# Seven block products of sums in place of eight in most of a SwiGLU down projection

## The chip, the cores and the metric

The kernel runs on one core of a Trainium2 chip. The metric is the device time of one execution in microseconds. The kernel before takes 1716.26 us, the median of three runs (1715.64 to 1716.47).

## The reference

One decoder layer on 256 tokens of width 2048, in float32. Two SwiGLU feed-forward networks (FFNs) of width 5632 stand before and behind a mixer (attention and convolution side by side). Each of the three ends in a residual sum and a layer norm.

```python
def swiglu_ffn(x, w_gate, w_up, w_down):
    h = jax.nn.silu(x @ w_gate) * (x @ w_up)
    return h @ w_down
...
x = layer_norm(ALPHA * x + 0.5 * swiglu_ffn(x, ffn1_w_gate, ffn1_w_up, ffn1_w_down), ln1_g, ln1_b)
u = x @ w_in + b_in
...
x = layer_norm(ALPHA * x + mixed, ln2_g, ln2_b)
x = layer_norm(ALPHA * x + 0.5 * swiglu_ffn(x, ffn2_w_gate, ffn2_w_up, ffn2_w_down), ln3_g, ln3_b)
```

The change touches `h @ w_down` alone: (256 x 5632) by (5632 x 2048).

## The kernel before, in words

**Numbers as two parts.** To keep close to float32 accuracy, every operand is split into `hi`, its rounding to the fp32r type, and `lo`, the rest. `mm3` (line 465) makes a product as three matmuls into one PSUM bank: hi by hi, hi by lo, lo by hi. ScalarE casts `hi` (line 133), and VectorE, or GpSimd for the sources in the set `pooled`, subtracts to get `lo` (line 135).

**Weights.** All weights come as a list of sources, each 128 rows by 1024 columns of float32 (512 KB). `Steps` works through the list: `load` issues DMAs on SP's queue into four `raw` buffers, `split` turns the oldest raw source into `hi` and `lo` (rings of 8, `RING`), `take` hands the next pair to a product, `release` says that TensorE is past it. `step` is called after each source's matmuls; it runs what was put off with `at`, and `ahead(2)` splits up to two more sources, at most 7 ahead of the last one taken (`LEAD`). Each engine runs its instructions in the order in which this Python code issues them.

**An FFN.** `ffn` (line 646) cuts the 5632 inner columns, 44 tiles of 128, into two parts of 24 and 20 (`JA`). For each part it first makes `h`: `token_group` (line 490) takes 8 sources for two tiles, gate and up columns side by side, and accumulates both blocks of 128 tokens in the banks of `psB` and `psC`, 96 matmuls. `group` (line 652) then applies SiLU on ScalarE (line 658) and the product on VectorE (line 659), and over the next steps transposes the result in blocks of 32 (line 666) and splits it into `hh` and `hl` (lines 670, 671).

**The down product.** `tokens_by` (line 584) then goes through the four chunks of 512 output columns. In each it takes the part's sources one by one; a source holds two of the part's tiles (rows of `w_down`) by 512 columns, and gives 12 matmuls: two tiles, two blocks of tokens, three matmuls each. At the end of a chunk `evacuate` (line 291) adds half the sum, from PSUM, onto the residual rows in `xt` (line 299, VectorE). In the last part the second block of tokens is held back by `SKEW` 6 or, at the very end of the kernel, `LAST` 8 sources, so that the layer norm of the first block runs under the products of the second.

The mixer in the middle has its own products; there GpSimd makes most of the `lo` parts, while VectorE runs convolution taps (line 852).

Of the kernel before, what the change touches and what calls it, by code (L numbers as in the profile page):

```python
# [9 lines left out]
F32 = mybir.dt.float32  # L10
F32R = mybir.dt.float32r
# [3 lines left out]
ALU = mybir.AluOpType  # L15
# [3 lines left out]
P = 128  # L19
D = 2048  # L20
S = 256
DFF = 5632
KT = D // P
JT = DFF // P
JA = 24
JG = 2
NC_ = D // 512
HD = 64
# [9 lines left out]
RING = 8  # L38
# [14 lines left out]
ZB = 5  # L53
# [11 lines left out]
class Steps:  # L65
# [6 lines left out]
    def __init__(self, nc, pool, sources, head, pooled, xT, x_raw, xcat):  # L72
        self.nc, self.pool, self.sources, self.head, self.pooled = nc, pool, sources, head, pooled
        self.xT, self.x_raw, self.xcat = xT, x_raw, xcat
        self.loaded = self.open = self.whole = self.done = self.used = self.now = 0
        self.jobs, self.ready = [], {}
        self.later, self.background, self.backlog = [], None, 0.0
        self.most = len(sources)

        n = KT // 2  # L80
        self.order = [g * n + t for t in range(TURNS) for g in range(2)]
        self.order += [g * n + t for g in range(2) for t in range(TURNS, n)]
# [19 lines left out]
    def load(self):  # L102
        while self.open < RAW_BUFS and self.loaded < len(self.sources):
            n = self.loaded
            if n < 4:

                raws = [self.raw(), self.raw()]
                self.get_x(n, 2)
                for q in range(2):
                    for i in range(2):  # L110
                        self.get(raws[i], n + i, q * 512, 512)
                self.jobs += [("free", None, None)] * 2
                continue
            raw = self.raw()
# [3 lines left out]
            self.jobs.append(("free", None, None))  # L118

    def split(self):  # L120
        nc = self.nc
        n, raw, at = self.jobs.pop(0)
        if n is None:
            nc.scalar.copy(at[:, :, 0, :], raw)
            nc.vector.tensor_tensor(out=at[:, :, 1, :], in0=raw, in1=at[:, :, 0, :].bitcast(F32), op=ALU.subtract)
        else:
            if n not in self.ready:
                self.ready[n] = [
                    self.pool.tile([P, 1024], F32R, tag=t, name=f"{t}{n}", bufs=RING) for t in ("hi", "lo")
                ]  # L130
            cols = slice(at, at + raw.shape[1])
            hi, lo = (t[:, cols] for t in self.ready[n])
            nc.scalar.copy(hi, raw)  # L133
            eng = nc.gpsimd if n in self.pooled else nc.vector
            eng.tensor_tensor(out=lo, in0=raw, in1=hi.bitcast(F32), op=ALU.subtract)  # L135
            if eng is nc.vector:
                self.vector(1.16, 1.3)
            if cols.stop == 1024:
                self.whole = n + 1
        while self.jobs and self.jobs[0][0] == "free":  # L140
            self.jobs.pop(0)
            self.open -= 1
            self.load()

    def ahead(self, most):
        while most > 0 and self.jobs:
            n = self.jobs[0][0]
            if n is not None and n >= min(self.used + LEAD, self.done + RING, self.most):
                break
            self.split()  # L150
            most -= 1

    def take(self):
        n = self.used
        self.used += 1
        while n >= self.whole:
            self.split()
        return self.ready.pop(n)

    def release(self):  # L160
# [6 lines left out]
    def at(self, delay, work, after=False):  # L167
        self.later.append((self.now + delay, after, work))
# [31 lines left out]
def hybrid_layer(  # L200
# [3 lines left out]
    nc = tc.nc  # L204
# [11 lines left out]
    sources = []  # L216

    def add_ffn(wu, wd):
        for j0, j1 in ((0, JA), (JA, JT)):
            for g in range(j0 // JG, j1 // JG):  # L220
                sources.extend(wu[g, q, h] for q in range(4) for h in range(2))
            for c in range(NC_):
                sources.extend(wd[c, g, h] for g in range(j0 // 4, j1 // 4) for h in range(2))

    add_ffn(wu1, wd1)
    first = len(sources)
# [10 lines left out]
    xt = act.tile([P, 2, D], F32, tag="xt", name="xt")  # L237
# [227 lines left out]
    def mm3(ps, s_hi, s_lo, m_hi, m_lo, start, stop):  # L465
        nc.tensor.matmul(ps, s_hi, m_hi, start=start, stop=False)  # L466
        nc.tensor.matmul(ps, s_hi, m_lo, start=False, stop=False)  # L467
        nc.tensor.matmul(ps, s_lo, m_hi, start=False, stop=stop)  # L468
# [115 lines left out]
    def tokens_by(lhs, k0, nk, factor, stats, finish, kept=None, lag=0):  # L584
# [36 lines left out]
        for n, (c, t, w) in enumerate(held):  # L621
# [21 lines left out]
                finish(1)  # L643
            st.step()

    def ffn(xc, tag, skew, begun, prepare, finish, kept=None):
        with tc.tile_pool(name=f"ffn{tag}", bufs=2) as pool:
            for part, (j0, j1) in enumerate(((0, JA), (JA, JT))):
                n = j1 - j0
                hh = pool.tile([P, JA, S], F32R, tag="hh", name=f"hh{part}", bufs=1)  # L650
                hl = pool.tile([P, JA, S], F32R, tag="hl", name=f"hl{part}", bufs=1)
                def group(j, ps, hh=hh, hl=hl):

                    ht = pool.tile([P, 2, JG * P], F32, tag="ht", name="ht")
                    hf = pool.tile([P, JG, S], F32, tag="hf", name="hf")
                    for b in range(2):
                        sl = pool.tile([P, JG * P], F32, tag="sl", name="sl")
                        nc.scalar.activation(sl, ps[b][:, : JG * P], AF.Silu)  # L658
                        nc.vector.tensor_tensor(out=ht[:, b], in0=sl, in1=ps[b][:, JG * P :], op=ALU.mult)  # L659

                    def turn(f):

                        for t in range(4):
                            src = ht[32 * t : 32 * t + 32].rearrange("p b (j f n) -> p f b j n", j=JG, n=32)
                            dst = hf[32 * f : 32 * f + 32].rearrange("p j (b t n) -> p t b j n", b=2, n=32)
                            nc.vector.transpose(dst[:, t], src[:, f])  # L666

                    def split():
                        js = slice(j, j + JG)
                        nc.scalar.copy(hh[:, js], hf)  # L670
                        nc.vector.tensor_tensor(out=hl[:, js], in0=hf, in1=hh[:, js].bitcast(F32), op=ALU.subtract)

                    for f in range(4):
                        st.at(1 + f, lambda f=f: turn(f), True)
                    st.at(5, split, True)
# [12 lines left out]
                if part == 1:  # L688
                    prepare(pool)
                stats = new_stats(f"st{tag}", 1 if kept is None else 2) if part == 1 else None  # L690
                tokens_by((hh, hl), 0, n, 0.5, stats, (lambda b: finish(b, stats)) if part == 1 else None,
                          kept if part == 1 else None)

    def params(name):
        return small.tile([P, 2, 4], F32, tag=name, name=name, bufs=1)
# [19 lines left out]
    rows3, kept = [], {}  # L715
# [4 lines left out]
    def prepare3(pool):  # L720

        nc.scalar.activation(small.tile([P, 1], F32, tag="rs_v", name="rs_s"), eps, AF.Sqrt)
        for c in range(NC_):
            g = pool.tile([P, 512], F32, tag="g3", name=f"g3{c}", bufs=NC_)
# [409 lines left out]
```

## Time and profile before

| | before |
|---|---|
| median of the runs | 1716.26 us |
| the profiled execution, first to last instruction | 1713.9 us |
| busy: TensorE matmuls | 1702.6 us, 99% |
| busy: VectorE | 1183.7 us, 69% |
| busy: ScalarE | 808.7 us, 47% |
| busy: GpSimd | 206.2 us, 12% |
| `lo` of weights on VectorE | 543 instructions, 660.4 us |
| `lo` of weights on GpSimd | 73 instructions, 175.9 us |
| matmuls | 7857 recorded, of them 2124 in the FFN down products |

How to read it: the profiled execution is 2.4 us shorter than the median of the runs, since a run has a little around the first and last instruction. Matmuls are pipelined, so their busy times overlap; what one costs is the stretch of a stage divided by its count. An engine's line in the trace gives the start, the length, the engine, the line of the kernel, the operation, what it writes and reads by the program's names, and in brackets how long the engine was idle before and what ended that.

In the trace the parts follow each other as up stage and down stage; the first down stage lies at 266.2 to 396.9 us.

### The profile page before, as it was taken

How to read it: one execution, taken by the hardware profiler on the slowest of the kernel's cores; microseconds unless marked ns; L12 is line 12 of the kernel's file. 1: busy time of each engine (PE TensorE's matmuls, PEld its weight loads, DVE VectorE, ACT ScalarE, POOL GpSimd, SP SyncE). 2: the span in 40 equal slices, each digit the busy share in tenths (PEclk: the TensorE clock that was granted, in tenths of full speed). 3: DMA queues.
4: the chain of work that ended last, by engine and by line, in shares of the span. 5: the costliest groups of instructions: out<-in, count | busy, mean ns of one | idle time of the engine just before them, and what ended most of it. 6: DMA issues, size and time to landing. Idle time of an engine off the chain costs nothing.

```text
span 1713.9 us, 21604 instructions
## 1 busy us (share of the span) xinstructions
PE 1702.6 (99%) x7857; PEld 1416.3 (83%) x7857; DVE 1183.7 (69%) x2021; ACT 808.7 (47%) x1044; POOL 206.2 (12%) x116
## 2 busy tenths in 40 slices
PE   9999999999999999999999999999999999999997
PEld 7888888888888888888888888888888888888886
DVE  7877776545777765658888788877764467777655
ACT  6544444334444443477665465444443344444431
POOL 0000000000000000168996200000000000000000
PEclk9999999999999999999999999999999999999999
DMA  9766655666656656555754557655556656665662
GB/s 317 259 205 194 195 191 192 196 196 190 193 195 195 191 191 196 170 176 190 203 178 159 196 187 244 209 196 192 192 189 201 194 190 195 196 193 191 233 206 75
DMA packets 96299, 336.38 MB, mean 196 GB/s; under 512 B 11200, under 2 KB 11328, under 8 KB 95936
## 3 DMA queue, kind: packets, MB, share of 16 engines
q1 hardware_dynamic: 96048, 334.74, 60.7%
q8 instruction: 61, 1.00, 0.2%
q14 instruction: 46, 0.38, 0.1%
q10 hardware_dynamic: 144, 0.26, 0.0%
HBM read 332.86 MB, written 2.10 MB: 195 GB/s over the span
## 4 chain that ended last, share of the span: by engine, by line
PE 99%; DVE 0%; DMA 0%; ACT 0%; issue 0%; DVEq 0%; SPq 0%
PE grp L468 18%; PE grp L467 18%; PE grp L466 18%; PE acc L466 11%; PE acc L467 11%; PE acc L468 11%; PE in_c L789 2%; PE in_a L789 2%; PE in_q L789 1%; PE in_a L787 1%; PE in_c L787 1%; PE grp L487 1%; PE grp L488 1%; PE grp L485 1%; PE in_q L787 1%; PE tp L339 0%
## 5 line engine op out<-in xcount | busy, mean ns | idle before, releaser
L133 ACT CAST hi<-raw 128x1024 fp32r<-128x1024 f32 (+1 forms) x616 | 643.0, 1047 | 762.7 <-PE grp L468 357.9
L135 DVE TENSOR_TENSOR lo<-raw,hi 128x1024 fp32r<-128x1024 f32 (+1 forms) x543 | 660.4, 1221 | 386.2 <-ACT hi L133 382.1
L466 PE MATMUL grp<-hi,xcat 128*128 128x512 f32 x1384 | 538.4, 389 | 0.0
L467 PE MATMUL grp<-lo,xcat 128*128 128x512 f32 x1384 | 538.4, 389 | 0.0
L468 PE MATMUL grp<-hi,xcat 128*128 128x512 f32 x1384 | 538.4, 389 | 0.0
L467 PEld LDWEIGHTS grp<-lo,xcat 128*128 128x128 f32 x1384 | 259.8, 188 | 54.1
L466 PEld LDWEIGHTS grp<-hi,xcat 128*128 128x128 f32 x1384 | 259.8, 188 | 53.9
L468 PEld LDWEIGHTS grp<-hi,xcat 128*128 128x128 f32 x1384 | 259.8, 188 | 53.8
L466 PE MATMUL acc<-hi,hh 128*128 128x512 f32 x708 | 274.7, 388 | 0.0
L468 PE MATMUL acc<-hi,hl 128*128 128x512 f32 x708 | 274.6, 388 | 0.0
L467 PE MATMUL acc<-lo,hh 128*128 128x512 f32 x708 | 274.6, 388 | 0.0
L135 POOL TENSOR_TENSOR lo<-raw,hi 128x1024 fp32r<-128x1024 f32 x73 | 175.9, 2432 | 730.3 <-ACT hi L133 723.4
L666 DVE STREAM_TRANSPOSE hf<-ht 32x128 f32<-32x128 f32 x704 | 212.8, 302 | 11.2
L466 PEld LDWEIGHTS acc<-hi,hh 128*128 128x128 f32 x708 | 132.9, 188 | 27.3
L467 PEld LDWEIGHTS acc<-lo,hh 128*128 128x128 f32 x708 | 132.9, 188 | 27.2
L468 PEld LDWEIGHTS acc<-hi,hl 128*128 128x128 f32 x708 | 132.9, 188 | 27.2
L852 DVE SCALAR_TENSOR_TENSOR conv<-hc,cw_sb,conv 128x256 f32<-128x256 f32 x231 | 96.7, 485 | 1.1
L449 POOL TENSOR_SCALAR rs_t<-rs_y,rs_w 128x1 f32<-128x1 f32 x1 | 0.3, 342 | 717.9 <-DVE rs_y L448 717.9
L299 DVE SCALAR_TENSOR_TENSOR xt<-acc,xt 128x512 f32<-128x512 f32 x46 | 31.7, 690 | 54.7 <-PE acc L468 54.7
L658 ACT ACTIVATE sl<-grp 128x256 f32<-128x256 f32 x88 | 33.6, 384 | 56.5 <-PE grp L468 52.7
L466 PE MATMUL acc<-hi,mh 128*128 128x512 f32 x128 | 50.5, 394 | 0.0
L659 DVE TENSOR_TENSOR ht<-sl,grp 128x256 f32<-128x256 f32 x88 | 36.5, 418 | 20.3 <-ACT sl L658 20.2
(149 smaller groups left out, 947.6 us busy)
## 6 DMA issues: line engine op xcount, KB each, us to landing
raw<-in_wu SPq DMA_DIRECT2D x348, 512.0 KB, 4.3
raw<-in_wd SPq DMA_DIRECT2D x176, 512.0 KB, 4.3
raw<-in_win SPq DMA_DIRECT2D x52, 512.0 KB, 4.0
raw<-in_wout SPq DMA_DIRECT2D x32, 512.0 KB, 4.0
xt<-in_xT SPq DMA_DIRECT2D x8, 256.0 KB, 5.8
raw<-in_head SPq DMA_DIRECT2D x8, 256.0 KB, 4.7
xt<-in_x SPq DMA_DIRECT2D x2, 1024.0 KB, 8.0
rg<-in_rows SPq DMA_DIRECT2D x8, 256.0 KB, 4.4
```

Source lines behind the costliest of these rows:

```text
L133: nc.scalar.copy(hi, raw)
L135: eng.tensor_tensor(out=lo, in0=raw, in1=hi.bitcast(F32), op=ALU.subtract)
L299: nc.vector.scalar_tensor_tensor(out=y, in0=ps, scalar=factor, in1=x_, op0=ALU.mult, op1=ALU.add)
L466: nc.tensor.matmul(ps, s_hi, m_hi, start=start, stop=False)
L467: nc.tensor.matmul(ps, s_hi, m_lo, start=False, stop=False)
L468: nc.tensor.matmul(ps, s_lo, m_hi, start=False, stop=stop)
L658: nc.scalar.activation(sl, ps[b][:, : JG * P], AF.Silu)
L659: nc.vector.tensor_tensor(out=ht[:, b], in0=sl, in1=ps[b][:, JG * P :], op=ALU.mult)
L666: nc.vector.transpose(dst[:, t], src[:, f])
L787: nc.tensor.matmul(ps[:, :S], w[1][:, n], x1[:, k, 0, :], start=False, stop=k == KT - 1)
L789: nc.tensor.matmul(ps, w[0][:, n], x1[:, k], start=k == 0, stop=False)
L852: nc.vector.scalar_tensor_tensor(out=out, in0=x_, scalar=w, in1=acc, op0=ALU.mult, op1=ALU.add)
```

## The change

The 44 tiles are cut into parts of 16, 16 and 12 (`PARTS`). The last part runs as before. In the first two, `by_sums` takes the place of `tokens_by`. It goes through two chunks of output columns at a time, so that a row pair of `w_down` (two tiles) by two chunks is a 2 x 2 block matrix, and `h` for two tiles by two token blocks is another. A plain pair ("C") makes the eight block products, accumulating four results. A set ("S") uses Strassen's scheme in Winograd's form: seven products, of block sums of `h` by block differences of the weights. Four of the seven are accumulated over the sets of the chunk pair in banks of their own (1, 5, 6, 7), three in banks that the plain pairs use too (2, 3, 4), and a bank 0 is for plain pairs alone: all eight banks. The order is C S S C S S S C.

The block sums of `h` (four per set) are made once in `group`, on VectorE, and split there, the `lo` on GpSimd. The weight differences are made for every set: `load_set` loads the two sources, `first` splits the first (`lo` on GpSimd), `rest` makes four differences of 512 columns on VectorE, two sources whose `lo` is VectorE's, and one of half the width whose `lo` is GpSimd's. After the last set of a chunk pair `shared` combines the banks that belong to sets alone: one scaled copy on ScalarE, four additions from PSUM on VectorE, four additions onto `xt` on GpSimd. The other four banks are added to `xt` at the end. `ht` and `hf` have one buffer in place of two, and the scale rows of the last norm use another tag.

```diff
-JA = 24
+PARTS = ((0, 16), (16, 32), (32, 44))
+KINDS = ("CSSCSSSC", "CSSCSSSC", None)
...
+    def load_set(self, n):
+
+        raws = [self.raw(), self.extra.tile([P, 1024], F32, tag="rawx", name=f"rawx{n}", bufs=2)]
+        self.opened += 1
+        self.loaded += 3
+        for raw, src in zip(raws, self.sources[n][0]):
+            self.nc.sync.dma_start(raw, src)
+        self.jobs += [(n, raws, self.first), (n + 3, raws, self.rest)]
+
+    def upper(self, n, raw):
+
+        pair = [self.pool.tile([P, 1024], F32R, tag=t, name=f"{t}{n}", bufs=RING) for t in ("hi", "lo")]
+        hi, lo = (t[:, : raw.shape[1]] for t in pair)
+        self.nc.scalar.copy(hi, raw)
+
+        def lower(eng):
+            eng.tensor_tensor(out=lo, in0=raw, in1=hi.bitcast(F32), op=ALU.subtract)
...
+    def first(self, n, raws):
+        self.upper(n, raws[0])(self.nc.gpsimd)
+
+    def rest(self, last, raws):
+
+        n = last - 2
+        a, b = ([r[:, :512], r[:, 512:]] for r in raws)
+        sub = self.nc.vector.tensor_tensor
+        self.flush(1)
+        t = self.extra.tile([P, 1024], F32, tag="sum", name=f"sum{n}", bufs=1)
+        sub(out=t[:, :512], in0=b[0], in1=a[0], op=ALU.subtract)
+        sub(out=t[:, 512:], in0=b[1], in1=t[:, :512], op=ALU.subtract)
+        one = self.upper(n, t)
+        sub(out=b[0], in0=b[1], in1=b[0], op=ALU.subtract)
+        two = self.upper(n + 1, raws[1])
+        self.flush()
+        sub(out=a[1], in0=a[1], in1=t[:, 512:], op=ALU.subtract)
+        self.vector(2.4, 0.3)
+        self.upper(n + 2, a[1])(self.nc.gpsimd)
+        self.open -= 1
...
+        self.pending = [lambda: one(self.nc.vector), ended]
...
+            def shared():
+
+                tmp.update((k, act.tile([P, 512], F32, tag="z", name="part", bufs=ZB)) for k in range(4))
+                nc.scalar.mul(tmp[0], bank[1], factor)
+                add(tmp[1], 6, tmp[0])
+                add(tmp[3], 5, tmp[1])
+                add(ys[1, 1], 5, ys[1, 1])
+                add(tmp[2], 7, tmp[1])
+                for n, (at, k) in enumerate((((0, 0), 0), ((0, 1), 3), ((1, 0), 2), ((1, 1), 2))):
+                    st.at(n + 2, lambda y=ys[at], t=tmp[k]: nc.gpsimd.tensor_tensor(
+                        out=y, in0=y, in1=t, op=ALU.add
+                    ), True)
...
+                if kind == "S":
+                    u = [st.take() for _ in range(2)]
+                    product(1, a, u[0], 0)
+                    product(5, a + 3, u[1], 0)
+                    product(6, a + 4, u[1], 1)
+                    u.append(st.take())
+                    product(7, a + 5, u[2], 0)
+                    st.step(2.7)
+                    product(2, a + 2, u[0], 1)
+                    st.release()
+                    st.release()
+                    product(3, a + 6, u[2], 1)
+                    st.release()
+                    u.append(st.take())
+                    product(4, a + 1, u[3], 0)
+                    st.release()
+                    if t == final:
+                        shared()
+                    st.step(2.0)
...
+                        for o, x_, y, op in (
+                            (0, h4[:, 0], h4[:, 2], ALU.add), (2, h4[:, 1], h4[:, 0], ALU.subtract),
+                            (1, s4[:, 0], h4[:, 1], ALU.subtract), (3, h4[:, 3], s4[:, 1], ALU.subtract),
+                        ):
+                            nc.vector.tensor_tensor(out=s4[:, o], in0=x_, in1=y, op=op)
+                        parted(a, h4[:, 1:], nc.gpsimd)
+                        parted(a + 3, s4, nc.gpsimd)
```

The two `lo` of `rest` that VectorE makes are put off (`pending`) and issued one by one in the next steps, after which the next set's load is issued.

More of the change, by code (lines that the diff above doesn't have):

```diff
@@ L24 @@
 JT = DFF // P
-JA = 24
+PARTS = ((0, 16), (16, 32), (32, 44))
+KINDS = ("CSSCSSSC", "CSSCSSSC", None)
+BLOCKS = {"S": 7, "C": 4}
 JG = 2
@@ L74, in __init__ @@
         self.xT, self.x_raw, self.xcat = xT, x_raw, xcat
-        self.loaded = self.open = self.whole = self.done = self.used = self.now = 0
-        self.jobs, self.ready = [], {}
+        self.loaded = self.open = self.opened = self.whole = self.done = self.used = self.now = 0
+        self.jobs, self.ready, self.pending = [], {}, []
         self.later, self.background, self.backlog = [], None, 0.0
@@ L113, in load @@
                 continue
+            if isinstance(self.sources[n], tuple):
+                if self.opened == 2:
+                    return
+                self.load_set(n)
+                continue
             raw = self.raw()
@@ L118, in load, with flush, ended @@
             self.jobs.append(("free", None, None))
+    def load_set(self, n):
[11 more added lines that the diff above has]
+            eng.tensor_tensor(out=lo, in0=raw, in1=hi.bitcast(F32), op=ALU.subtract)
+            if eng is self.nc.vector:
+                self.vector(1.16, 1.3)
+            self.ready[n] = pair
+            while self.whole in self.ready:
+                self.whole += 1
+        return lower
+    def flush(self, most=9):
+        while most > 0 and self.pending:
+            self.pending.pop(0)()
+            most -= 1
+    def first(self, n, raws):
[16 more added lines that the diff above has]
+        self.open -= 1
+        def ended():
+            two(self.nc.vector)
+            self.opened -= 1
+            self.load()
+        self.pending = [lambda: one(self.nc.vector), ended]
     def split(self):
         nc = self.nc
+        if not self.jobs:
+            return self.flush()
         n, raw, at = self.jobs.pop(0)
-        if n is None:
+        if callable(at):
+            at(n, raw)
+            self.load()
+        elif n is None:
             nc.scalar.copy(at[:, :, 0, :], raw)
@@ L133, in split @@
             nc.scalar.copy(hi, raw)
+            self.flush()
             eng = nc.gpsimd if n in self.pooled else nc.vector
@@ L148, in ahead @@
             if n is not None and n >= min(self.used + LEAD, self.done + RING, self.most):
+                self.flush(most)
                 break
@@ L156, in take @@
         while n >= self.whole:
-            self.split()
+            if self.pending:
+                self.flush(1)
+            else:
+                self.split()
         return self.ready.pop(n)
@@ L218, in add_ffn @@
     def add_ffn(wu, wd):
-        for j0, j1 in ((0, JA), (JA, JT)):
+        for (j0, j1), kinds in zip(PARTS, KINDS):
             for g in range(j0 // JG, j1 // JG):
                 sources.extend(wu[g, q, h] for q in range(4) for h in range(2))
-            for c in range(NC_):
-                sources.extend(wd[c, g, h] for g in range(j0 // 4, j1 // 4) for h in range(2))
+            pairs = [divmod(t, 2) for t in range(j0 // 2, j1 // 2)]
+            if kinds is None:
+                sources.extend(wd[c, g, h] for c in range(NC_) for g, h in pairs)
+                continue
+            for c in range(0, NC_, 2):
+                for kind, (g, h) in zip(kinds, pairs):
+                    both = (wd[c, g, h], wd[c + 1, g, h])
+                    sources.extend(both if kind == "C" else [(both, i) for i in range(4)])
     add_ffn(wu1, wd1)
@@ L644, in tokens_by, with by_sums, product, add @@
             st.step()
+    def by_sums(hh, hl, kinds, factor):
+        firsts = [sum(BLOCKS[k] for k in kinds[:t]) for t in range(len(kinds))]
+        final = kinds.rindex("S")
+        for c in range(0, NC_, 2):
+            one, seven = (p.tile([P, 512], F32, tag="acc", name="sum") for p in (psB, psC))
+            mid = psA.tile([P, 2, 512], F32, tag="gu", name="sum")
+            two, four = (p.tile([P, 512], F32, tag="acc", name="sum") for p in (psB, psC))
+            end = psA.tile([P, 2, 512], F32, tag="gu", name="sum")
+            bank = {1: one, 7: seven, 5: mid[:, 0], 6: mid[:, 1], 2: two, 4: four, 3: end[:, 0], 0: end[:, 1]}
+            uses = {k: kinds.count("S") for k in (1, 5, 6, 7)}
+            uses |= {k: kinds.count("S") + 2 * kinds.count("C") for k in (2, 3, 4)} | {0: 2 * kinds.count("C")}
+            left = dict(uses)
+            ys = {(i, j): xt[:, 1 - i, (c + j) * 512 : (c + j + 1) * 512] for i in range(2) for j in range(2)}
+            tmp = {}
+            def product(k, block, w, half):
+                cols = slice(half * 512, (half + 1) * 512)
+                left[k] -= 1
+                mm3(
+                    bank[k], hh[:, block], hl[:, block], w[0][:, cols], w[1][:, cols],
+                    left[k] == uses[k] - 1, left[k] == 0,
+                )
+            def add(out, k, other):
+                nc.vector.scalar_tensor_tensor(
+                    out=out, in0=bank[k], scalar=factor, in1=other, op0=ALU.mult, op1=ALU.add
+                )
+                st.vector(0.66, 0.3)
+            def shared():
[9 more added lines that the diff above has]
+                    ), True)
+            for t, kind in enumerate(kinds):
+                a = firsts[t]
+                ends = t == len(kinds) - 1
+                if kind == "S":
[17 more added lines that the diff above has]
+                    st.step(2.0)
+                else:
+                    for i, (p, q) in enumerate(((2, 4), (3, 0))):
+                        w = st.take()
+                        for k, blocks in ((p, (1, 3)), (q, (0, 2))):
+                            for half in range(2):
+                                product(k, a + blocks[half], w, half)
+                        st.release()
+                        if ends:
+                            for k, at in ((p, (0, i)), (q, (1, i))):
+                                add(ys[at], k, ys[at])
+                        st.step()
+                if ends and kind == "S":
+                    for k, at in ((2, (0, 0)), (4, (1, 0)), (3, (0, 1)), (0, (1, 1))):
+                        if uses[k]:
+                            add(ys[at], k, ys[at])
@@ L646, in ffn, with group @@
     def ffn(xc, tag, skew, begun, prepare, finish, kept=None):
         with tc.tile_pool(name=f"ffn{tag}", bufs=2) as pool:
-            for part, (j0, j1) in enumerate(((0, JA), (JA, JT))):
+            st.extra = pool
+            for part, ((j0, j1), kinds) in enumerate(zip(PARTS, KINDS)):
                 n = j1 - j0
[L650 to L655, printed above, removed]
+                ends = part == len(PARTS) - 1
+                blocks = 2 * n if kinds is None else sum(BLOCKS[k] for k in kinds)
+                hh, hl = (pool.tile([P, blocks, P], F32R, tag=t, name=f"{t}{part}", bufs=1) for t in ("hh", "hl"))
+                def group(j, ps, hh=hh, hl=hl, kinds=kinds):
+                    ht = pool.tile([P, 2, JG * P], F32, tag="ht", name="ht", bufs=1)
+                    hf = pool.tile([P, JG, S], F32, tag="hf", name="hf", bufs=1)
@@ L687, in ffn @@
                     j += JG
[L688 to L692, printed above, removed]
+                if kinds is not None:
+                    by_sums(hh, hl, kinds, 0.5)
+                    continue
+                prepare(pool)
+                stats = new_stats(f"st{tag}", 1 if kept is None else 2)
+                lhs = [x_.rearrange("p (j b) n -> p j (b n)", b=2) for x_ in (hh, hl)]
+                tokens_by(lhs, 0, n, 0.5, stats, lambda b: finish(b, stats), kept)
     def params(name):
@@ L723, in prepare3 @@
         for c in range(NC_):
-            g = pool.tile([P, 512], F32, tag="g3", name=f"g3{c}", bufs=NC_)
+            g = act.tile([P, 512], F32, tag="z", name=f"g3{c}", bufs=ZB)
             nc.sync.dma_start(g, rows[5, c * 512 : (c + 1) * 512].partition_broadcast(P))
```

15 lines of the change are left out of this document (11 added, 4 removed).

## The prediction

> **What bounds the kernel now.** I read the page first: busy time of each engine, the slices of GpSimd, the chain that ended last.
>
> ```profile
> span 1713.9 us, 21604 instructions
> ...
> PE 1702.6 (99%) x7857; PEld 1416.3 (83%) x7857; DVE 1183.7 (69%) x2021; ACT 808.7 (47%) x1044; POOL 206.2 (12%) x116
> ...
> POOL 0000000000000000168996200000000000000000
> ...
> PE 99%; DVE 0%; DMA 0%; ACT 0%; issue 0%; DVEq 0%; SPq 0%
> ```
>
> TensorE is the chain from end to end; the others have room on average, and GpSimd works only in the mixer, in the middle. So a matmul saved is time saved, unless something else becomes late. That is decided in the changed stage, so I took busy time by windows: an up stage, the first down stage, and that down stage's products alone.
>
> ```profile
> 100.00:209.00 109.00, 109.00 (x482) 90.31 (x481) 79.72 (x137) 48.04 (x55) 0.00 (x0) 1.00 0.61 194
> 266.20:396.90 130.70, 130.70 (x578) 108.28 (x577) 67.78 (x73) 51.42 (x50) 0.00 (x0) 1.00 0.61 194
> ...
> 266.20:396.90 130.70, 130.68 (x576) 107.92 (x575) 4.84 (x7) 1.00 0.61 194
> ```
>
> After the length come TensorE, its weight loads, VectorE, ScalarE, GpSimd (the third line has the first three), then clock, DMA share, GB/s. A down matmul takes 130.68/576 = 0.227 us; a source of 1024 columns feeds 12 of them, 2.72 us. VectorE is half busy in the down stage and GpSimd idle there.
>
> **What is saved.** A row pair over two output chunks was 2 sources, 8 products of 3 matmuls: 24 x 0.227 = 5.44 us. As a set of seven products it is 21 x 0.227 = 4.76 us. Five sets, 2 chunk pairs, 2 parts, 2 FFNs, 3 matmuls each: 120 matmuls, 27.2 us. With TensorE still the bound, a part of 16 tiles goes from 384 x 0.227 = 87.1 us to 354 x 0.227 = 80.3 us.
>
> **What is added to the other engines.** The durations:
>
> ```profile
> L133 ACT CAST hi<-raw 128x1024 fp32r<-128x1024 f32 (+1 forms) x616 | 643.0, 1047 | 762.7 <-PE grp L468 357.9
> ...
> L671 DVE TENSOR_TENSOR hl<-hf,hh 128x512 fp32r<-128x512 f32 x44 | 30.2, 685 | 0.0
> L299 DVE SCALAR_TENSOR_TENSOR xt<-acc,xt 128x512 f32<-128x512 f32 x46 | 31.7, 690 | 54.7 <-PE acc L468 54.7
> L403 POOL TENSOR_TENSOR xt<-xt,rb 128x512 f32<-128x512 f32 x8 | 10.5, 1314 | 0.0
> ...
> 264.77 1.23 DVE L135 TENSOR_TENSOR lo<-raw,hi 128x1024 fp32r<-128x1024 f32 x1 [1.50 <-ACT hi L133]
> 265.91 0.42 DVE L659 TENSOR_TENSOR ht<-sl,grp 128x256 f32<-128x256 f32 x1
> ...
> 268.91 1.24 DVE L666 STREAM_TRANSPOSE hf<-ht 32x128 f32<-32x128 f32 x4
> ```
>
> On VectorE the next instruction starts 0.09 us before the last ends (264.77 + 1.23 against 265.91), so in a row a 1024-wide `lo` costs 1.14 and a 512-wide one 0.60 us. A plain row pair costs VectorE 2 x 1.14 = 2.28. A set costs it four 512-wide differences and two `lo`: 4.7 us. GpSimd gets per set one 1024-wide `lo` and one of 512. ScalarE has 3.5 casts, 3.7 us, under a set's 4.76, and stays hidden.
>
> If VectorE and GpSimd ran freely side by side, all of it would hide: per chunk pair VectorE has 5 x 4.7 + 3 x 2.28 + 8 evictions x 0.60 = 35.1 us against TensorE's 40.1. Whether they do is the crux. Both inputs of every added difference and `lo` lie in SBUF, on both engines. In the mixer the two are busy together, and I looked there, first at taps whose running sum lies in PSUM, then at VectorE instructions with both inputs in SBUF.
>
> ```profile
> 814.36 4.77 POOL L135 TENSOR_TENSOR lo<-raw,hi 128x1024 fp32r<-128x1024 f32 x2
> 816.19 4.79 DVE L852 SCALAR_TENSOR_TENSOR conv<-hc,cw_sb,conv 128x256 f32<-128x256 f32 x12
> ...
> 937.01 2.41 POOL L135 TENSOR_TENSOR lo<-raw,hi 128x1024 fp32r<-128x1024 f32 x1
> 937.75 2.22 DVE L1021 TENSOR_TENSOR ml<-sw,mh 128x512 fp32r<-128x512 f32 x1 [2.31 <-ACT mh L1020]
> ...
> 943.17 2.40 POOL L135 TENSOR_TENSOR lo<-raw,hi 128x1024 fp32r<-128x1024 f32 x1
> 944.75 1.91 DVE L135 TENSOR_TENSOR lo<-raw,hi 128x1024 fp32r<-128x1024 f32 x1 [3.58 <-ACT hi L133]
> 945.54 3.38 POOL L135 TENSOR_TENSOR lo<-raw,hi 128x1024 fp32r<-128x1024 f32 x1
> 947.80 2.21 DVE L135 TENSOR_TENSOR lo<-raw,hi 128x1024 fp32r<-128x1024 f32 x1 [1.14 <-ACT hi L133]
> ```
>
> The taps run at 0.40 us each beside GpSimd, undisturbed. The others take turns: GpSimd ends at 939.42, the 512-wide VectorE one at 939.97, 0.55 later; GpSimd ends at 945.57, `lo` at 946.66, 1.09 later; and GpSimd's next, begun at 945.54, stretches to 3.38 and ends 2.26 after VectorE let go. The wait goes both ways and each runs its full length alone. In the changed stage their times add.
>
> One set in order: GpSimd's 1024 (2.26), VectorE's next difference (0.55), two more (1.20), two `lo` (2.28), GpSimd's 512 (1.16, an estimate: 1.31 less the 0.15 by which 2.41 shrinks to 2.26), the next set's first difference (0.55): 8.0 us, where TensorE needs 4.76. Behind a difference that waits for GpSimd stand, on VectorE, the other differences and both `lo`; for these wait products 5 and 6, then 7, 2 and 3, and SP's next load of the pair. DMA stays hidden: 1.05 MB per 8.0 us is 131 GB/s, under the 194 shown.
>
> The Trainium skill (SBUF — State Buffer, Who interferes with whom) has this as a lock that whoever starts first holds for the whole instruction, the other blocked. By whole profiled durations a set would be 4 x 0.69 + 2 x 1.23 + 2.41 + 1.31 = 8.9 us, and the kernel some 37 us later than by my sum; the trace agrees with the lock, but shows 0.09 to 0.15 us less per instruction.
>
> **The sum for one part of 16 tiles.** Per chunk pair: five sets 40.0, three plain pairs 6.84, the four GpSimd additions of shared parts 4 x 1.16 = 4.64, the eight evictions 4.8, which read PSUM and so may run beside GpSimd; I hide half, 2.4. Together 53.9, twice 107.8.
> - Done before the stage begins, thanks to the lead of 7 sources: the first plain pair 2.28 and about 6.0 of the first set's 8.0 (it is issued two steps of 2.72 ahead): -8.3.
> - Not needed before the last set is ready: the last plain pair 2.28, four additions 4.64, half the evictions 2.4: -9.3.
> - The last up group's 16 transposes, 4 x 1.25 = 5.0, which have one input and half hide, and a split 0.60: +3.1.
> - After the last `lo` TensorE has 4 products left, 2.7, and a plain pair, 5.44: +8.2.
>
> That is 101.5 us against 87.1: +14.4 per part, +57.6 for four. The profiled span of 1713.9 becomes 1771.5; the median of the runs is 2.4 above the span, so 1774.
>
> Both ends: perfectly interleaved (7.8 a set, evictions and transposes hidden, 12.3 us done ahead: 2.28, the whole first set, the next one's 2.26) a part takes 90.0, +11.6 in all, 1728. With whole durations (8.9 a set) and nothing hidden, 115.4, +113, 1830. I stay between: VectorE issues in order, so it cannot always fill.
>
> **Priced at nothing.** Up stage: 79.72/5 = 15.9 us of VectorE per group of 21.8. In 5 groups of each part the block sums add four 128-wide operations (each under the 0.42 of the 256-wide one), take one of 0.69 away, and bring two GpSimd splits of at most 1.31 to wait for: at most 3.6 more, 19.5, which the group covers; without that cover it would cost up to 20 x 3.6 = 72 us. Single `ht`, `hf` buffers: rewritten a group later, 21.8 us. Scale rows in another tag: the same four loads. The last part of 12 tiles, with its held products now reaching into the third chunk: one eviction, 0.69, under 8 held steps of 6 x 0.227 = 1.36. At each part's start the first product reuses the last group's bank, free at 265.91 + 0.42, 0.2 us late; TensorE is not what is late there.
>
> **Rivals.**
> Faster: the two engines do not get in each other's way much, because GpSimd's instructions fall into VectorE's pauses. Then TensorE bounds: 1713.9 - 27.2 + about 5 (eight chunk-pair ends where the eviction of the last two banks stands behind a set's differences, 0.6 each) = 1692, run 1694. For it: 35.1 under 40.1. Against it: the sum of locked work, at least 50.5 per chunk pair, has no room in 40.1. It decides where a set falls to (40.1 - 13.9)/5 = 5.2 us. Chance 0.13.
> No change: the lead covers 14 us per part more than I allow. 0.03.
> Much slower: TensorE pauses 8.0 - 4.76 = 3.2 us in each set, and its clock drops. The windows show clock 1.00 without a pause, so nothing here prices it. Were its rate to halve in them, the sets would take 5 x 9.5 + 3 x 5.44 = 63.8 per chunk pair, 127.6 per part, +162: about 1880. Chance 0.05. The Trainium skill (TensorE: Matmul & The Clock Gate, What's actually happening) halves the clock after an idle window of about 3.4 us; by that rule this pause just misses it. No run here shows that yet.
>
> **How the numbers follow.** Forecast, taking turns, 1728 to 1830: 0.79. With the rivals: slower 0.84, same 0.03, faster 0.13; 0.2% (3.4 us) is about what can be told from no change. The range is the forecast's own; it leaves out the fast and the throttled case and takes the sign as settled.
>
> **What would show it.** Right: VectorE `lo` and differences in the two parts stretched to about 2 us and GpSimd's 1024-wide ones to over 3; a set every 8 us; TensorE waiting for VectorE's `lo`, 20 to 25 us per part, 354 matmuls in it; the up stages and the 12-tile parts unchanged. Wrong: TensorE busy throughout, GpSimd's `lo` at 2.4 and VectorE's at 1.23 there. If the parts take near 80 us, taking turns was misjudged; if above 116, the clock or another wait is in it.

## The result and the profile after

The changed kernel takes 1781.65 us, the median of four runs (1777.87 to 1785.36); the kernel before takes 1715.99 in its four. The ratio is 1.038, with a 95% interval of 1.036 to 1.040: slower, as forecast, 7.7 us above the forecast of 1774. One of the four executions of the kernel with three sets, further down, took 3984.57 us at full clock; its median counts it, its ratio does not. The page of the profile, with the lines that answer to those of before:

```profile
span 1781.5 us, 22148 instructions
...
PE 1712.0 (96%) x7737; PEld 1404.6 (79%) x7737; DVE 1462.4 (82%) x2289; ACT 872.4 (49%) x1152; POOL 491.8 (28%) x268
...
POOL 0101462001454000168997201023611023620000
PEclk9999999999989999999999999999899999999999
...
PE 81%; DVE 13%; issue 3%; ACT 1%; DMA 1%; POOL 0%; DVEq 0%; ACTq 0%; SPq 0%
```

The 120 matmuls are gone (7857 to 7737 recorded), yet PE is busy longer than before. GpSimd's row has four new humps, the four changed parts, and VectorE now stands on the chain for 13% of the span where it had 0. One up stage, one changed part and the up stage behind it, by windows (stretch and its length, TensorE, weight loads, VectorE, ScalarE, GpSimd, clock, DMA share, GB/s):

```profile
100.00:180.00 80.00, 80.00 (x354) 66.28 (x353) 65.19 (x112) 36.09 (x44) 12.62 (x9) 1.00 0.59 194
179.90:283.10 103.20, 87.86 (x356) 68.01 (x355) 98.50 (x97) 46.69 (x54) 47.23 (x22) 0.95 0.43 150
283.10:457.00 173.90, 173.90 (x769) 144.04 (x768) 140.18 (x223) 80.34 (x94) 23.98 (x17) 1.00 0.62 201
```

In the part, VectorE is busy for 98.5 of 103.2 us and TensorE pauses for 15.3; in the up stages TensorE never pauses. From first to last product the four changed parts take 103.3, 103.6, 103.6 and 103.4 us, against 87.1 for 16 tiles before: 65.5 of the 67.6 us by which the span grew. The list of waits puts TensorE's pauses in the first part down to VectorE's `lo` (6.9 us), ScalarE's casts (4.4), GpSimd's `lo` (2.6) and a VectorE addition (1.4). What "busy" means on VectorE is in the timeline of one set, VectorE's rows first and then GpSimd's (start, length), and of the place where the shared sums of the first chunk pair are added:

```profile
200.62 1.22 DVE L143 TENSOR_TENSOR lo<-rawx,hi 128x1024 fp32r<-128x1024 f32 x1
201.76 1.78 DVE L167 TENSOR_TENSOR sum<-rawx,raw 128x512 f32<-128x512 f32 x1
203.57 2.75 DVE L168 TENSOR_TENSOR sum<-rawx,sum 128x512 f32<-128x512 f32 x1
206.25 0.68 DVE L170 TENSOR_TENSOR rawx<-rawx 128x512 f32<-128x512 f32 x1
206.85 0.68 DVE L173 TENSOR_TENSOR raw<-raw,sum 128x512 f32<-128x512 f32 x1
207.51 1.23 DVE L143 TENSOR_TENSOR lo<-sum,hi 128x1024 fp32r<-128x1024 f32 x1
208.66 1.22 DVE L143 TENSOR_TENSOR lo<-rawx,hi 128x1024 fp32r<-128x1024 f32 x1
209.79 1.79 DVE L167 TENSOR_TENSOR sum<-rawx,raw 128x512 f32<-128x512 f32 x1
...
201.00 2.00 POOL L143 TENSOR_TENSOR lo<-raw,hi 128x512 fp32r<-128x512 f32 x1 [3.26 <-ACT hi L140]
202.95 2.83 POOL L143 TENSOR_TENSOR lo<-raw,hi 128x1024 fp32r<-128x1024 f32 x1
...
239.20 5.07 POOL L766 TENSOR_TENSOR xt<-xt,part 128x512 f32<-128x512 f32 x3
```

Read the ends, not the starts. The `lo` in the first row ends at 201.84; GpSimd's 512 ends at 203.00, 1.16 later; the first difference at 203.54, 0.54 later; GpSimd's 1024 at 205.78, 2.24 later; the second difference at 206.32, 0.54 later. Each waits for the other's whole instruction, and the wait is recorded as busy: two operations that take 0.68 us undisturbed show 1.78 and 2.75. The next set begins 8.03 us after this one.

### The profile page after: what moved, and what is told of

It reads as the page before. It is cut to its first block, busy times and chain, and to the rows that moved or that the text cites. A ratio compares the mean times of both kernels' runs of the same rounds, so it can differ in the third digit from the quotient of the medians.

```text
span 1781.5 us, 22148 instructions
## 1 busy us (share of the span) xinstructions
PE 1712.0 (96%) x7737; PEld 1404.6 (79%) x7737; DVE 1462.4 (82%) x2289; ACT 872.4 (49%) x1152; POOL 491.8 (28%) x268
## 4 chain that ended last, share of the span: by engine, by line
PE 81%; DVE 13%; issue 3%; ACT 1%; DMA 1%; POOL 0%; DVEq 0%; ACTq 0%; SPq 0%
PE grp L547 18%; PE grp L549 18%; PE grp L548 18%; PE acc L547 4%; PE acc L549 4%; PE acc L548 4%; DVE sum L168 4%; DVE lo L143 2%; DVE sum L167 2%; PE sum L548 2%; PE sum L549 2%; PE sum L547 2%; PE in_c L972 2%; PE in_a L972 2%; PE in_q L972 1%
## 5 line engine op out<-in xcount | busy, mean ns | idle before, releaser
L203 ACT CAST hi<-raw 128x1024 fp32r<-128x1024 f32 (+1 forms) x536 | 553.1, 1044 | 425.2 <-PE grp L549 174.3
L206 DVE TENSOR_TENSOR lo<-raw,hi 128x1024 fp32r<-128x1024 f32 (+1 forms) x463 | 590.6, 1293 | 181.1 <-ACT hi L203 176.3
L143 POOL TENSOR_TENSOR lo<-raw,hi 128x1024 fp32r<-128x1024 f32 x80 | 180.6, 2265 | 262.9 <-ACT hi L140 255.1
L206 POOL TENSOR_TENSOR lo<-raw,hi 128x1024 fp32r<-128x1024 f32 x73 | 176.0, 2437 | 248.2 <-ACT hi L203 241.3
L548 PE MATMUL sum<-lo,hh 128*128 128x512 f32 x472 | 196.0, 415 | 37.2 <-DVE lo L143 27.6
L547 PE MATMUL sum<-hi,hh 128*128 128x512 f32 x472 | 193.3, 409 | 19.9 <-ACT hi L140 16.6
L549 PE MATMUL sum<-hi,hl 128*128 128x512 f32 x472 | 191.1, 405 | 0.0
L548 PEld LDWEIGHTS sum<-lo,hh 128*128 128x128 f32 x472 | 93.3, 198 | 68.9 <-DVE lo L143 34.0
L547 PEld LDWEIGHTS sum<-hi,hh 128*128 128x128 f32 x472 | 92.7, 196 | 49.5 <-ACT hi L140 29.6
L549 PEld LDWEIGHTS sum<-hi,hl 128*128 128x128 f32 x472 | 93.5, 198 | 18.9
L168 DVE TENSOR_TENSOR sum<-rawx,sum 128x512 f32<-128x512 f32 x40 | 77.3, 1932 | 1.4
```

Source lines behind the costliest of these rows:

```text
L168: sub(out=t[:, 512:], in0=b[1], in1=t[:, :512], op=ALU.subtract)
```

## The experiments

The theory: VectorE's instructions with two inputs in SBUF and GpSimd's that read SBUF take turns, so that in the changed parts their times add. The rivals: VectorE's own load is too much, whatever GpSimd does; or it is the recut, or something else in the new order. Each kernel is compared with runs of the kernel before on its own chip (medians 1716.1 to 1716.4).

**The change without the collision.** GpSimd keeps its place and nearly its busy time, but only writes: three fills in place of each subtraction and each addition in the changed parts. It leaves out those `lo` parts and additions, so it prices and is no version to use.

```diff
+            if eng is self.nc.gpsimd:
+                for _ in range(3):
+                    eng.memset(lo.bitcast(F32), 0.0)
...
-                    st.at(n + 2, lambda y=ys[at], t=tmp[k]: nc.gpsimd.tensor_tensor(
-                        out=y, in0=y, in1=t, op=ALU.add
-                    ), True)
+                    st.at(n + 2, lambda t=tmp[k]: [
+                        nc.gpsimd.memset(t, 0.0) for _ in range(3)
+                    ], True)
```

> GpSimd stays busy at the same places, but only writes: three memsets stand for each lo of a set and for each addition of the shared parts. Left out: those lo are zero, the shared parts are not added. Theory (it is GpSimd's reading of SBUF that shuts out VectorE's two-input instructions): VectorE runs at full rate, TensorE bounds the part at 80.3 us plus a little, 81 to 84; total about 1696 us. Rival (VectorE is late by its own work, or the order of the work and the loads set the pace): about 1780 us as in the changed kernel. Second rival (any busy GpSimd, a writing one too, shuts VectorE out): also about 1780.

Measured: 1690.69, ratio 0.985 [0.984, 0.987]. The first changed part by windows:

```profile
178.90:259.40 80.50, 80.50 (x356) 66.65 (x356) 75.58 (x101) 48.59 (x55) 48.42 (x74) 1.00 0.58 196
```

and its timeline, a set's first differences beside a GpSimd fill:

```profile
203.68 0.69 DVE L171 TENSOR_TENSOR sum<-rawx,raw 128x512 f32<-128x512 f32 x1
204.40 0.69 DVE L172 TENSOR_TENSOR sum<-rawx,sum 128x512 f32<-128x512 f32 x1
...
202.75 1.70 POOL L145 MEMSET lo<- 128x512 f32 x3 [0.42 <-PE sum L552]
```

GpSimd is as busy as in the changed kernel (48.4 against 47.2), VectorE still has all its differences, and TensorE never pauses. What costs is GpSimd's reading, 91 us in all. Then one input in place of two: two copies of the source for each of GpSimd's subtractions (these `lo` parts hold the source instead).

```diff
+            if eng is self.nc.gpsimd:
+                for _ in range(2):
+                    eng.tensor_copy(lo, raw)
```

> The changed kernel, but GpSimd makes each of a set's lo by two copies of the raw tile, which read one SBUF input in place of two; the four additions stay. Left out: those lo hold the raw weights. Theory (whatever reads SBUF on GpSimd shuts VectorE's two-input instructions out): VectorE's differences are stretched by the copies' length, a part stays well over 87 us, total 1740 to 1790. Rival (only GpSimd instructions with two inputs do): stretched ones only at the additions, total 1692 to 1715.

Measured: 1754.35, ratio 1.022 [1.020, 1.024], a set in 7.18 us:

```profile
208.23 1.09 DVE L171 TENSOR_TENSOR sum<-rawx,raw 128x512 f32<-128x512 f32 x1
209.36 1.41 DVE L172 TENSOR_TENSOR sum<-rawx,sum 128x512 f32<-128x512 f32 x1
210.69 1.52 DVE L174 TENSOR_TENSOR rawx<-rawx 128x512 f32<-128x512 f32 x1
212.13 0.68 DVE L177 TENSOR_TENSOR raw<-raw,sum 128x512 f32<-128x512 f32 x1
...
208.73 1.50 POOL L145 CAST lo<-raw 128x1024 fp32r<-128x1024 f32 x1
210.29 1.38 POOL L145 CAST lo<-raw 128x1024 fp32r<-128x1024 f32 x1
```

One input read by GpSimd is enough to hold VectorE up. The Trainium skill (SBUF — State Buffer, Who interferes with whom) has it so: VectorE's second SBUF input comes through the interface that GpSimd reads by, and a GpSimd instruction that only writes does not contend. Both runs agree.

**All of it on VectorE.** If turns are what costs, GpSimd's work done by VectorE should cost less, since VectorE needs 1.14 us for a `lo` that holds it up for 2.24.

```diff
-        self.upper(n, raws[0])(self.nc.gpsimd)
+        self.upper(n, raws[0])(self.nc.vector)
...
-        self.upper(n + 2, a[1])(self.nc.gpsimd)
+        self.upper(n + 2, a[1])(self.nc.vector)
...
-                    st.at(n + 2, lambda y=ys[at], t=tmp[k]: nc.gpsimd.tensor_tensor(
+                    st.at(n + 2, lambda y=ys[at], t=tmp[k]: nc.vector.tensor_tensor(
```

> GpSimd's work in the down stage of the first two parts (two lo per set, four additions per chunk pair) goes to VectorE; nothing is left out. Theory (the two engines take turns, their times add): a set falls from 8.0 to 4 x 0.60 + 3.5 x 1.14 = 6.4 us, a chunk pair from about 54 to 46, a part from 103.4 to about 89 us; total about 1726 us, so some 55 us faster than the changed kernel although its busiest engine gets more to do. Rival (VectorE alone is too slow, GpSimd's help is real): 1.7 us more per set and 2.4 per chunk pair on VectorE, 40 x 1.7 + 8 x 2.4 = 89 us more, about 1870 us.

Measured: 1793.63, ratio 1.045 [1.044, 1.047]: a miss by 68 us and slower than the changed kernel. Its waits in the first part (total, times, longest):

```profile
DVE lo L143 <- ACT hi L140: 13.8, 12, 1.5
```

The edit makes a new wait. The half-wide source is made by `rest`'s last difference, and its `lo` stands right behind it; VectorE idles until ScalarE has cast it. So the third `lo` was put behind the two that were waiting, as `three(self.nc.vector)` in `ended`:

```diff
-        self.upper(n + 2, a[1])(self.nc.vector)
+        three = self.upper(n + 2, a[1])
...
             two(self.nc.vector)
+            three(self.nc.vector)
```

> As the run with all of it on VectorE, but the half-wide fourth lo of a set is issued behind the other two, so that VectorE need not wait for ScalarE's cast of it (13.8 us of such waits per part in that run). Nothing is left out. Theory (VectorE is the bound there, at 6.4 us per set without waits): a part falls from 105.9 to about 92 us, total about 1738 us, so 44 us under the changed kernel with GpSimd idle. Rival (VectorE's issue order was no cause, the added VectorE work as such costs it): stays at about 1790 us.

Measured: 1773.53, ratio 1.033 [1.032, 1.035], again a miss, now by 36. The same view:

```profile
DVE lo L143 <- ACT hi L140: 7.5, 5, 2.4
...
DVE lo L207 <- ACT hi L204: 2.8, 2, 1.6
```

Now it is the next set's first `lo`, issued ahead of those put off, whose cast comes late. The third form issues it behind them:

```diff
     def first(self, n, raws):
-        self.upper(n, raws[0])(self.nc.vector)
+        one = self.upper(n, raws[0])
+        self.flush()
+        one(self.nc.vector)
```

> Five sets, all of GpSimd's down-stage work on VectorE, each lo issued in the order in which ScalarE's casts end (the next set's first lo behind this set's last). Nothing left out. Theory: VectorE without waits takes 6.4 us a set; the last such run had 10.5 us of waits for ScalarE in a part of 100.7, so a part falls to about 90 us, total about 1731 us, 50 under the changed kernel though GpSimd does nothing. Rival (some other limit sets the set's length once GpSimd is idle): stays near 1773 us.

Measured: 1738.33, ratio 1.013 [1.011, 1.014]; the first part, and three sets' first differences:

```profile
179.10:271.40 92.30, 84.34 (x356) 67.34 (x355) 87.05 (x117) 44.38 (x52) 0.00 (x0) 0.98 0.46 163
```

```profile
196.09 0.68 DVE L169 TENSOR_TENSOR sum<-rawx,raw 128x512 f32<-128x512 f32 x1
...
202.71 0.68 DVE L169 TENSOR_TENSOR sum<-rawx,raw 128x512 f32<-128x512 f32 x1
...
209.33 0.68 DVE L169 TENSOR_TENSOR sum<-rawx,raw 128x512 f32<-128x512 f32 x1
```

The same arithmetic, with GpSimd idle in the part, is 43 us faster than with its help; a set takes 6.62 us in place of 8.03. That is still over TensorE's 4.76, so the first rival holds in part: five sets are too many for VectorE even alone.

**Fewer sets.** If a set costs VectorE 8 us and a plain pair 2.3, there is a number of sets at which TensorE bounds again. Three of eight, GpSimd still helping:

```diff
-KINDS = ("CSSCSSSC", "CSSCSSSC", None)
+KINDS = ("CSCCSCSC", "CSCCSCSC", None)
```

> Order C S C C S C S C: three sets in place of five, nothing left out. Theory (taking turns): a chunk pair's turns are 3 x 8.0 + 5 x 2.28 + 4.64 + 2.4 = 42.4 us against TensorE's 41.5, with the lead a part is bound by TensorE at 83.0 plus 1 to 2; total about 1704 us, faster than both kernels. Rival (the cost goes with the number of sets, whatever the room between them): three fifths of 66 us remain, about 1755 us.

Measured: 1701.74, ratio 0.992 [0.990, 0.994]. Four sets, GpSimd helping:

```diff
-KINDS = ("CSSCSSSC", "CSSCSSSC", None)
+KINDS = ("CSCSSCSC", "CSCSSCSC", None)
```

> The changed kernel with four sets, order C S C S S C S C, GpSimd's work where the change puts it; nothing left out. Theory (taking turns, 8.0 us a set): 4 x 8.04 + 4 x 2.28 + 4.64 + 2.4 = 48.3 us per chunk pair, a part 2 x 48.3 - 8.3 - 9.3 + 3.1 + 8.2 = 90.3 us, total about 1729 us: already slower than before, where three sets were faster. Rival (cost per set, no threshold): halfway between three and five sets, 1742 us. If TensorE still bounded: 81.6 us a part, 1696 us.

Measured: 1733.72, ratio 1.011 [1.009, 1.012]. The same `KINDS` with all the edits of the second form above, everything on VectorE:

> The same with four sets in place of five, order C S C S S C S C; nothing left out. Theory: VectorE 4 x 6.42 + 4 x 2.28 + 2.4 + 4.8 = 42.0 us per chunk pair against TensorE's 40.8, the lead of about 7 us covers the rest: a part at 82 to 85 us, total 1696 to 1708, faster than before. Rival (each set costs its share whatever the room): between the five-set and the no-set run, above 1720 us.

Measured: 1733.97, ratio 1.011 [1.009, 1.013], missed through the same late casts (VectorE is busy for 80.9 of a part's 91.0 us). The same with the third form's `first`:

> The same with four sets, order C S C S S C S C. Theory: VectorE 42.0 us per chunk pair against TensorE's 40.8, the lead covers it, a part at 82 to 84 us, total about 1702 us, as good as three sets with GpSimd. Rival (other waits stay): 1715 to 1734 us.

Measured: 1709.69, ratio 0.996 [0.995, 0.998], between the 1702 of the theory and the 1715 at which its rival begins. The same four sets with `first` unchanged, so that GpSimd keeps the first `lo` of a set, and VectorE has the rest:

```diff
-        self.upper(n + 2, a[1])(self.nc.gpsimd)
+        three = self.upper(n + 2, a[1])
...
+            three(self.nc.vector)
...
-                    st.at(n + 2, lambda y=ys[at], t=tmp[k]: nc.gpsimd.tensor_tensor(
+                    st.at(n + 2, lambda y=ys[at], t=tmp[k]: nc.vector.tensor_tensor(
```

> Four sets; GpSimd keeps only the 1024-wide first lo of a set, the half-wide lo and the additions go to VectorE. Theory (taking turns): 2.26 + 2.35 + 2.28 + 0.60 = 7.5 us a set, 4 x 7.5 + 9.12 + 2.4 + 2.4 = 43.9 per chunk pair, a part 83.7 us, total about 1703 us; between the four-set run with all of it on GpSimd (1734 us) and the bound by TensorE (1695 us). Rival (the turns are not what sets four sets' time): stays at about 1734 us.

Measured: 1725.65, ratio 1.005 [1.004, 1.007], a miss by 23. The first parts of three sets, four with GpSimd, four on VectorE, and the mixed four:

```profile
179.30:262.50 83.20, 83.20 (x368) 68.88 (x367) 76.52 (x82) 41.21 (x46) 31.59 (x14) 1.00 0.58 196
```

```profile
179.40:271.50 92.10, 85.61 (x362) 68.29 (x361) 85.12 (x89) 42.59 (x49) 38.90 (x18) 0.98 0.49 167
```

```profile
179.30:264.60 85.30, 82.95 (x362) 67.38 (x361) 80.05 (x107) 42.58 (x49) 0.00 (x0) 1.00 0.53 182
```

```profile
179.30:268.80 89.50, 85.15 (x362) 68.56 (x361) 83.34 (x101) 43.28 (x50) 18.66 (x7) 0.98 0.51 176
```

At three sets TensorE's busy time fills the part: a part has 18 matmuls fewer than a plain one, and their time comes out (83.1 us from first to last product, against 87.2 with plain products alone, below). It is the fastest complete version measured, faster than both kernels. At four the part is longer by what VectorE cannot do in time, and it is shorter with GpSimd out of the way. The mixed four failed in two terms. VectorE's last `lo` for a set ends 79.7 us behind the part's first product. Up to there VectorE is busy or blocked for 75.1 us, where the expected 83.7, less a tail of 8.2 as in the prediction, leaves 75.5; but it is idle for 4.7 more, of which the list of waits puts 4.1 down to casts and SiLU of ScalarE. The rest is TensorE's tail behind that `lo`, 9.7 us. Whether another order of those casts would bring it back was not tried.

**Single terms.** The four additions of each chunk pair on VectorE, and no other edit:

```diff
-                    st.at(n + 2, lambda y=ys[at], t=tmp[k]: nc.gpsimd.tensor_tensor(
+                    st.at(n + 2, lambda y=ys[at], t=tmp[k]: nc.vector.tensor_tensor(
```

> The changed kernel with the four additions of the shared parts on VectorE in place of GpSimd, all else as the change puts it; nothing left out. Theory: per chunk pair 4 x 1.16 us of GpSimd's turns become 4 x 0.60 of VectorE's own, 2.2 us less; 8 chunk pairs, 18 us, total about 1764 us. Rival (GpSimd's additions run beside VectorE for nothing): 8 x 2.4 = 19 us more, about 1801 us.

Measured: 1772.43, ratio 1.033 [1.032, 1.035], 9.2 us faster than the changed kernel, half of what was expected. In the trace of the changed kernel only four of a part's eight additions lie inside the part (234.18 to 244.27 in the first); the other four come behind the last product, where TensorE no longer waits for a set. The prediction's sum had left these four out; my expectation counted all eight. Three in a row on VectorE take 1.88 us here:

```profile
237.94 1.88 DVE L766 TENSOR_TENSOR xt<-xt,part 128x512 f32<-128x512 f32 x3
```

About 0.60 each: by turns, each of the four saves 1.16 - 0.60 = 0.56, and 4 x 4 x 0.56 is 9.0. The agreement is one of the total: in the profiled executions the four parts shrink by 3.5, 1.5, 1.8 and 1.5 us, where the turns alone give 2.2 each.

The recut alone, parts of 16, 16 and 12, all of them through `tokens_by`:

```diff
-KINDS = ("CSSCSSSC", "CSSCSSSC", None)
+KINDS = (None, None, None)
```

> Parts of 16, 16 and 12 tiles with plain products alone, no set; nothing left out. Theory: the new cut, the single buffers and the last part's shorter chunks cost nothing, 1716 us within 3. Rival: part of the 66 us lies in the cut (eight more evictions per FFN, a shorter lead), some us above 1719.

Measured: 1717.89, ratio 1.001 [1.000, 1.002]; a part of 16 tiles takes 87.2 us. By these runs the recut has no cost that can be told from none. One thing in its trace is new, though, and the changed kernel has it too: near the end of the last part TensorE waits for VectorE, which in the kernel before it doesn't:

```profile
PE acc L547 <- DVE st L386: 0.9, 1, 0.9
```

The row is the changed kernel's; with the recut alone the wait is 0.8.

## Why the prediction was right

**The saving** was there: with the collision taken out a part takes 80.4 us, against 80.3 worked out from 354 matmuls, and the kernel 1690.69, against 1694 for the rival in which TensorE bounds. The condition named against that rival, a set under 5.2 us, decided it: a set takes 8.03.

**Taking turns** is shown by three things: the ends in the timeline, the run in which GpSimd only writes, and the run in which GpSimd idles. The estimate from two places in the mixer held to 0.02 us: 0.54, 2.24 and 1.16 where the set was summed from 0.55, 2.26 and 1.16. The rule of the Trainium skill by whole durations, 8.9 us a set, overstates: an instruction shows its profiled length, but the other engine loses 0.09 to 0.17 us less. Of the signs named ahead, the differences that meet GpSimd stretched (1.78 and 2.75), and so did GpSimd's `lo`, the 1024-wide one a little less than "over 3" (2.83). VectorE's `lo` did not stretch to 2 us: in the set shown it takes 1.22. The sum had it so, at 1.14; the list of signs did not follow the sum.

**The part** was summed to 101.5 and takes 103.3. By the steps: VectorE's last `lo` for a set ends at 273.0, 93.2 us behind the part's first product, where the sum had 101.5 - 8.2 = 93.3. The stretch up to there by windows:

```profile
179.80:273.00 93.20, 77.86 (x318) 59.94 (x317) 89.78 (x88) 40.88 (x48) 46.18 (x22) 0.96 0.40 139
```

Inside that agreement one thing was not in the sum: VectorE idles for 3.4 of the 93.2 us, 2.9 of it waiting for ScalarE, so the charged work was too dear by as much. That the two errors cancel is luck; which charge was too dear was not traced. The term that missed is the tail, 10.1 us in place of 8.2 (9.9, 10.1 and 10.1 in the other three parts), and the trace shows why:

```profile
268.96 0.50 PE L548 MATMUL sum<-lo,hh 128*128 128x512 f32 x1 [0.66 <-POOL lo L143]
269.30 0.40 PE L549 MATMUL sum<-hi,hl 128*128 128x512 f32 x1
270.66 0.50 PE L547 MATMUL sum<-hi,hh 128*128 128x512 f32 x1 [0.97 <-ACT hi L140]
271.93 0.50 PE L548 MATMUL sum<-lo,hh 128*128 128x512 f32 x1 [0.76 <-DVE lo L143]
...
272.73 0.56 PE L548 MATMUL sum<-lo,hh 128*128 128x512 f32 x1
273.08 0.63 PE L549 MATMUL sum<-hi,hl 128*128 128x512 f32 x1
273.51 0.63 PE L547 MATMUL sum<-hi,hh 128*128 128x512 f32 x1
273.94 0.63 PE L548 MATMUL sum<-lo,hh 128*128 128x512 f32 x1
...
276.37 0.39 PE L548 MATMUL sum<-lo,hh 128*128 128x512 f32 x1
```

From 273.08 a matmul starts every 0.43 us in place of 0.227. The nine from 272.73 to 276.37 take 3.64 us in place of 9 x 0.227 = 2.04: 1.6 us of the tail's 1.9. The four parts together grew by 65.5 where the sum had 57.6, which is 7.9 of the 10.0 us between the forecast's span, 1771.5, and the profiled one; the other 2.1 lie outside the parts. Most of them seem to come with the recut: the kernel with the recut alone spans 1716.0, and on its chip the kernel before has a median span of 1714.6; 0.8 of the difference is the new wait in the last part. So small a difference lies within the interval above, so this is not shown.

**The clock**, then, did drop, which had a chance of 0.05. But it cost far less than that price: the part's window shows 0.95, not the rate of one half all through the sets that the price of 1880 took, and while VectorE sets the pace a slow matmul mostly fills a pause. That the drops inside the sets cost little is argued from VectorE's small idle time, not shown by a run of its own. They do not cost nothing: in the four runs the span grows as the mean clock falls (1776.1 us at 0.986, 1778.2 at 0.985, 1781.5 at 0.984, 1783.6 at 0.979). The prediction took a set's 3.2 us without matmuls for one pause, which just misses 3.4; away from the shared sums they come in pieces of at most 0.97 us, and the clock fell all the same (last section). The clock also explains the pauses: 20 to 25 us of TensorE waiting for VectorE's `lo` were forecast per part; 15.3 of pauses are there, 6.9 of them for that `lo`. The rest of the time lies in longer matmuls, since TensorE's busy time is 87.9 us for 354 of them that take 80.4 at full speed.

**What was priced at nothing** stayed so but for one term: the eight groups of the up stages between two changed parts take 21.8 us each, with TensorE busy in all of it. The one term is the last part, where the new wait of 0.9 us stands. DMA moves 150 GB/s in the part, under the 194 of the up stage.

Where my expectations of the experiments missed (the first two orders on VectorE, four sets with the second order, the mixed four), one error was in it each time: I summed VectorE's work and took the sum for the length, with no idle time. Each of these orders had casts of ScalarE that came late for an engine that issues in order.

## What to carry to other kernels

Before work is given to GpSimd because it idles, look for the places in the trace where it and the engine to be relieved both read SBUF: here its help with one `lo` held VectorE up for 2.24 us where VectorE needs 1.14, and taking the help away gained 43 us. A scheme that trades TensorE work for vector work should go no further than the other engine has time for: three sets in eight ran in 0.9915 [0.9895, 0.9935] of the time before, five in 1.0381 [1.0364, 1.0398]. When work moves onto an engine that issues in order, sum its waits for its inputs too: two orders of the same instructions differed by 35 us (1773.5 and 1738.3).

## What the runs showed of the hardware that was not expected

TensorE's clock halves without a long pause. In the 3.4 us before the slow stretch at 273 us the longest pause is 0.97 us, only the matmuls are sparse. The rows of the windows around the start of that stretch, and around another time at which the clock stayed up (the first number behind the length is TensorE's, the clock stands behind GpSimd's):

```profile
269.39:272.80 3.41, 1.68 (x7) 0.93 (x6) 3.41 (x5) 3.23 (x4) 0.64 (x1) 1.00 0.00 0
272.80:276.21 3.41, 3.41 (x10) 2.67 (x9) 3.36 (x3) 2.12 (x3) 1.35 (x1) 0.50 0.27 70
...
204.53:207.94 3.41, 1.95 (x7) 0.83 (x5) 3.41 (x4) 1.50 (x2) 1.25 (x1) 1.00 0.88 326
207.94:211.35 3.41, 2.65 (x12) 2.14 (x12) 3.41 (x3) 1.96 (x3) 2.32 (x2) 1.00 0.00 0
```

In the second row TensorE is busy throughout, at half speed. The four changed parts have eleven slow stretches, of 3.41 or 6.83 us, and they begin at whole multiples of 3.41 us from one another. So the trace can be cut into windows on that grid, as in the rows above. In each of the eleven windows ahead of a slow stretch TensorE is busy for between 0.50 and 1.81 us; the sparsest windows that no slow stretch follows show 1.79, 1.84, 1.90 and 1.95. In this kernel the limit thus lies near half of a window. It is not sharp: over the traces of all nine kernels here whose clock drops in the parts, every such window at full clock with under 1.5 us was followed by a slow stretch and none with 2 us or more, while between them both happened.

The Trainium skill (TensorE: Matmul & The Clock Gate, What's actually happening) lets the clock fall after an idle window of about 3.4 us. The length of the stretches fits that window. If idle means without a matmul, the condition does not fit: no pause shortly before 273 us comes near 3.4 us, and a window that is half busy was enough. The Trainium skill (TensorE: Matmul & The Clock Gate, A second HAM failure mode: psum-queue depth-cycling) tells of another kernel whose frequent short pauses made the clock swing, and that is what this trace looks like. With GpSimd helping, the first part's clock stays at 1.00 at three sets and shows 0.98 at four and 0.95 at five; with all of it on VectorE in the third order it is 1.00 at four and 0.98 at five.
